# Turning tokens to channels by SyncE transfers of 32-partition squares and two full-width transposes, with weight rows read in that order

## Chip, cores and metric

One core of one Trainium2 chip. The time is that of the device in microseconds (us), as the median of runs of the whole kernel. Engines are named as the profile names them: PE is TensorE, DVE is VectorE, ACT is ScalarE, POOL is GpSimd, SP is SyncE, the engine whose instruction queue issues nearly all transfers here.

## What is computed

One layer of a hybrid decoder block on 256 tokens with 2048 channels, in fp32. Three branches (windowed attention, a pooling mixer, a state-space mixer) come from one input projection, are projected back and merged by gates; an output projection, a gated feed-forward layer of 5632 channels and a last norm follow. Of the reference, the part that the change touches:

```
y = ssd(...)                                            # 256 x 2048
g = (y * silu(z)).reshape(b, l, 4, 512)
g = g * rsqrt(mean(g * g, -1) + EPS)
ssm = g.reshape(b, l, 2048) * ssm_norm_w
merged = gates0 * (att @ w_attn_br) + gates1 * (pool @ w_pool_br) + gates2 * (ssm @ w_ssm_br)
x = x + merged @ w_out
h2 = rmsnorm(x, ln2_w)
gu = h2 @ w_gate_up
x = x + (silu(gu[..., :D_FF]) * gu[..., D_FF:]) @ w_down
return rmsnorm(x, final_w)
```

## The kernel before

**Products.** A product is computed with tokens on the output partitions (`tokens_block`): the operand with channels on its partitions is the stationary side, 128 channels by 128 tokens, and the weights stream by in blocks of 512 columns. One block of a product over 2048 channels takes 16 channel tiles, k = 0 to 15. Precision comes from splitting both sides in a high and a low fp32r part; `three` issues three matmuls for each pair, high by high (L201), high by low weights (L202) and low operand by high weights (L203). With two token tiles that is 96 matmuls of 512 columns a block. The weights of a block come in four loads of 1 MB (`weights`, L150, tile `raw`, four buffers), four channel tiles each. Each load is split in two pieces: ACT rounds a piece to `whi` (L139), DVE subtracts to get `wlo` (L140). There are five buffers of `whi` and of `wlo`, so a piece is split when PE has left the fifth piece before it.

**Turns.** What comes out of a product has tokens on its partitions. Before it can be the operand of the next product it has to be turned, tokens to channels. For a block of 256 tokens by 512 channels (four channel tiles) `turn` does this on DVE: 16 stream transposes, each of 32 partitions by 256 elements (L347), into `tt`, then a split of `tt` into the high and low tiles of the operand. Where a norm's vector multiplies the operand the split is by channel tile with the vector as a per-partition factor (L142 on ACT, L143 on DVE). There are 23 turns: four of `y` into `ssm`, four of `m` into `mp`, four of `x2` into `x2p`, and eleven of `ff` into `f`, in three parts of 4, 4 and 3 blocks (`FF_PARTS`). The last turn of an operand gives its last four channel tiles: k = 12 to 15, or 8 to 11 in the third part.

**Order of work.** The program order on each engine is that of a scheduler which starts from the order of the code. A turn isn't put where it is written: its steps are `tasks` with a charge in microseconds (`later`), and each piece of a running product lets one task go when enough charge has been saved (`side`). `soon` makes two tasks of the squares where an operand is wanted early.

**After a turn.** `w_out` follows the branch product, four blocks (`mp` as operand); gate and up products follow, eight blocks for each part but the last (`x2p`), then the `down` products of the part (`f`). So the first block that uses an operand starts as soon as the block before it ends, and comes to the last four channel tiles after three loads.

Of the kernel before, what the change touches and what calls it, by code (L numbers as in the profile page):

```python
# [10 lines left out]
F32 = mybir.dt.float32  # L11
# [60 lines left out]
def hybrid_block(ctx: ExitStack, tc: tile.TileContext, ins, out):  # L72
# [13 lines left out]
    def k4(shape, dt=F32, name="k4"):  # L86
        return work.tile([P, *shape], dt, tag="k4", name=name, bufs=21)
# [29 lines left out]
    def later(fn, cost=0.0):  # L117
        tasks.append((fn, cost))
# [27 lines left out]
    def weights(loads, shape, pieces=2):  # L146

        raw = wpool.tile([P, *shape], F32, tag="raw", name="raw", bufs=4)
        for to, src in loads:
            sp.dma_start(to(raw), src)  # L150
        n, cols = shape
        parts = []
        for h in range(pieces):
            a, b = h * (n // pieces), (h + 1) * (n // pieces)
            hi = wpool.tile([P, b - a, cols], F32R, tag="whi", name="whi", bufs=5)
            lo = wpool.tile([P, b - a, cols], F32R, tag="wlo", name="wlo", bufs=5)
            split(raw[:, a:b], hi, lo)
# [20 lines left out]
    class Parts:  # L180

        def __init__(self, n, name):
            self.t = [
                (k4([4, SEQ], F32R, f"{name}_hi"), k4([4, SEQ], F32R, f"{name}_lo")) for _ in range(n // 4)
            ]

        def hi(self, k):
            return self.t[k // 4][0][:, k % 4, :]  # L190
# [14 lines left out]
    def tokens_block(a, nk, loads_of, cols, loaded=None):  # L205

        accs = [acc() for _ in range(T)]
        step = 8 if cols <= 256 else 4
        for i in range(0, nk, step):
            n = min(step, nk - i)  # L210
            pieces = weights(loads_of(i, n), [n, cols])
            if loaded is not None:
                loaded(i)
            for s, e, hi, lo in pieces:
                for t in range(T):
                    tok = slice(t * P, (t + 1) * P)
# [59 lines left out]
    vec = k2([2, P], F32, name="vec")  # L276
    r0 = 0
    VEC = {}
    for name, n in (("ln2_w", 16), ("ssm_norm_w", 16), ("pool_scale", 8), ("conv_b", 24)):
        VEC[name] = r0, n  # L280
        r0 += n
    n_vec = r0
# [52 lines left out]
                    last = split(p[:, k, :], dst.hi(kt), dst.lo(kt), scale(kt))  # L335
        return last

    def turn(block, k0, dst, scale=None, soon=False):

        tt = k4([4, SEQ], F32, "tt")  # L340
        src = block.rearrange("p t (k j c) -> p t k j c", k=4, j=4)
        to = tt.rearrange("p k (t i s) -> p t k i s", t=T, i=4)

        def squares(rows_):
            for i in rows_:
                for j in range(4):
                    dve.transpose(to[32 * j:32 * j + 32, :, :, i, :], src[32 * i:32 * i + 32, :, :, j, :])  # L347

        def parts():
            if scale is None:  # L350
                hi, lo = dst.t[k0 // 4]
                split(tt, hi, lo)
            else:
                for k in range(4):
                    split(tt[:, k, :], dst.hi(k0 + k), dst.lo(k0 + k), scale(k0 + k))

        if soon:
            later(lambda: squares((0, 1)), 2.0)
# [32 lines left out]
    upto_rows = dram.tile([T, SSM_HEADS, P], F32, name="upto_rows")  # L391
    rst = const.tile([P, SEQ], F32, name="rst")

    for name in ("ln2_w", "ssm_norm_w", "pool_scale", "conv_b"):
        vec_load(name)
    pool.dma_start(vec[:96, 1, :], ins["conv_w"][0].rearrange("k (a c) -> (k a) c", c=P))
    for i, name in enumerate(("dt_bias", "a_log", "d_skip")):
        pool.dma_start(heads[:, i, :], ins[name][0].partition_broadcast(P))
    pool.dma_start(sink, ins["attn_sink"][0].partition_broadcast(P))
    pool.dma_start(cst, ins["cst"][:, P:])  # L400


    def vdt_loads(i, n):
# [352 lines left out]
            act.activation(sg[:, t, :], a, AF.Sigmoid, scale=rstd1[:, t:t + 1])  # L756
        return sg

    def branch(br, j, a_parts, w, sg):
        if br == 0:  # L760
            m4.append(k4([T, NB], F32, "m"))
        nk = w.shape[0] // P
        for t, a in enumerate(tokens_block(a_parts, nk, plain_loads(w, 0, j * NB, NB), NB)):
            if br == 0:
                dve.tensor_tensor(m4[j][:, t, :], a, sg[:, t, :], ALU.mult)
            else:
                dve.tensor_tensor(sg[:, t, :], a, sg[:, t, :], ALU.mult)
                (dve if br == 2 else pool).tensor_tensor(m4[j][:, t, :], m4[j][:, t, :], sg[:, t, :], ALU.add)
# [63 lines left out]
    for g in range(GROUPS):  # L832
        for t, a in enumerate(tokens_block(h, KD, plain_loads(w_in, 0, C_Z + g * NB, NB), NB)):
            sz = k2([NB], F32, "sz")
            act.activation(sz, a, AF.Silu, scale=rstd1[:, t:t + 1])
            dve.tensor_tensor(ys[g][:, t, :], ys[g][:, t, :], sz, ALU.mult)
            junk = k2([NB], F32, "junk")
            act.activation(junk, ys[g][:, t, :], AF.Square, accum_out=ssg[:, t, g:g + 1])

        def finish(g=g):  # L840
            rstd = rsqrt(ssg[:, :, g], NB, [T], "rsg")
            for t in range(T):
                dve.tensor_scalar(ys[g][:, t, :], ys[g][:, t, :], rstd[:, t:t + 1], None, ALU.mult)

        later(finish, 1.5)
        turn(ys[g], 4 * g, ssm, lambda k: vcol("ssm_norm_w", k))

    sg_ssm = [gate(2, j) for j in range(2)]
    finish_tasks()
    for j in range(4):  # L850
        branch(2, j, ssm, ins["w_ssm_br"][0], sg_ssm[j])
        if j + 2 < 4:
            sg_ssm.append(gate(2, j + 2))
        if j == 1:
            mp = Parts(KD, "mp")
            for i in range(2):
                turn(m4[i], 4 * i, mp)
        elif j > 1:
            turn(m4[j], 4 * j, mp, soon=j == 3)


    x2 = []
# [4 lines left out]
    ss2 = tiny([T, 4], "ss2", 1)  # L867
    x2p = Parts(KD, "x2p")
    for j in range(4):
        for t, a in enumerate(tokens_block(mp, KD, plain_loads(ins["w_out"][0], 0, j * NB, NB), NB)):  # L870
            dve.tensor_tensor(x2[j][:, t, :], a, x2[j][:, t, :], ALU.add)
            junk = k2([NB], F32, "junk")
            act.activation(junk, x2[j][:, t, :], AF.Square, accum_out=ss2[:, t, j:j + 1])
        turn(x2[j], 4 * j, x2p, lambda k: vcol("ln2_w", k), soon=j == 3)
    ssum2 = tiny([T], "ssum2", 1)
    dve.tensor_reduce(ssum2, ss2, AX.X, ALU.add)
    rstd2 = rsqrt(ssum2, D, [T], "rs2")
# [21 lines left out]
    for some in FF_PARTS:  # L899
        f = Parts(4 * len(some), "f")  # L900
        for i, b in enumerate(some):
            a_ = k4([T, NB], F32, "ff")
            for t, a in enumerate(tokens_block(x2p, KD, plain_loads(wgu, 0, b * NB, NB), NB)):
                act.activation(a_[:, t, :], a, AF.Silu, scale=rstd2[:, t:t + 1])
            if b == FB - 1:

                act.activation(tiny([1], "junk1"), a_[:, 1, :1], AF.Square)
                act.activation(tiny([1], "junk1"), rstd2[:, :1], AF.Sqrt)
            for t, a in enumerate(tokens_block(x2p, KD, plain_loads(wgu, 0, DFF + b * NB, NB), NB)):
                dve.scalar_tensor_tensor(  # L910
                    a_[:, t, :], a, rstd2[:, t:t + 1], a_[:, t, :], ALU.mult, ALU.mult
                )
            turn(a_, 4 * i, f, soon=i == len(some) - 1)
        k0, nk = 4 * some[0], 4 * len(some)
        last = some[-1] == FB - 1
        for j in range(3 if last else 4):
            down(j, 0, NB, j if last else None, tokens_block(f, nk, plain_loads(wd, k0, j * NB, NB), NB))
    down(3, 0, 256, 3, tokens_block(f, nk, plain_loads(wd, k0, 3 * NB, 256), 256))


    wl = []
    for i in range(0, nk, 8):
        n = min(8, nk - i)
        raw = wpool.tile([P, n, 256], F32, tag="raw", name="raw", bufs=4)
        sp.dma_start(raw, rows(wd, k0 + i, n, 3 * NB + 256, 256))
        for b in range(0, n, 4):
            hi, lo = k4([4, 256], F32R, "wl_hi"), k4([4, 256], F32R, "wl_lo")
            split(raw[:, b:b + 4], hi, lo)
            wl.append((hi, lo))
# [53 lines left out]
```

## Time and profile before

| | |
|---|---|
| time, median of 3 runs | 1661.74 us (1661.23 to 1662.84) |
| the profiled execution: time, span | 1662.78 us, 1661.0 us |
| granted clock of PE in it | 0.998 |
| PE busy | 1645.3 us, 99%, 7815 matmuls |
| DVE busy | 1140.2 us, 69% |
| ACT busy | 823.6 us, 50% |
| POOL busy | 58.9 us, 4% |
| SP's transfers (queue q1) | 183872 packets, 309.87 MB, 56.5% of 16 DMA engines |

The span is that of the instructions of one execution; the time of the same execution is 1.8 us longer. Busy shares are means over stages that differ. A transfer counts for its queue, not for the engine that issues it, and SP's own time in issuing isn't in the table.

### The profile page before, as it was taken

How to read it: one execution, taken by the hardware profiler on the slowest of the kernel's cores; microseconds unless marked ns; L12 is line 12 of the kernel's file. 1: busy time of each engine (PE TensorE's matmuls, PEld its weight loads, DVE VectorE, ACT ScalarE, POOL GpSimd, SP SyncE). 2: the span in 40 equal slices, each digit the busy share in tenths (PEclk: the TensorE clock that was granted, in tenths of full speed). 3: DMA queues.
4: the chain of work that ended last, by engine and by line, in shares of the span. 5: the costliest groups of instructions: out<-in, count | busy, mean ns of one | idle time of the engine just before them, and what ended most of it. 6: DMA issues, size and time to landing. Idle time of an engine off the chain costs nothing.

```text
span 1661.0 us, 20077 instructions
## 1 busy us (share of the span) xinstructions
PE 1645.3 (99%) x7815; PEld 1372.4 (83%) x7815; DVE 1140.2 (69%) x1598; ACT 823.6 (50%) x1073; POOL 58.9 (4%) x58
## 2 busy tenths in 40 slices
PE   8999999999999999999999999999999999999997
PEld 7888888888888888888888888888888888888887
DVE  5789898955754469844898866665556666446675
ACT  5467678544444456644445544443344444344443
POOL 1000001200210000000000000000000000000000
PEclk9999999999999999999999999999999999999999
DMA  9654655556565645656575555556556655555552
GB/s 273 203 166 144 198 190 192 177 178 190 167 216 189 202 154 201 225 181 200 170 253 197 185 203 184 184 192 210 201 178 203 202 186 194 201 183 199 195 172 89
DMA packets 186271, 316.68 MB, mean 191 GB/s; under 512 B 7644, under 2 KB 59104, under 8 KB 186176
## 3 DMA queue, kind: packets, MB, share of 16 engines
q1 hardware_dynamic: 183872, 309.87, 56.5%
q0 software_dynamic: 1552, 4.66, 1.0%
q8 instruction: 61, 1.00, 0.2%
q10 hardware_dynamic: 752, 0.86, 0.2%
q14 instruction: 34, 0.28, 0.0%
HBM read 313.25 MB, written 2.13 MB: 190 GB/s over the span
## 4 chain that ended last, share of the span: by engine, by line
PE 94%; DVE 4%; ACT 1%; DMA 1%; issue 1%; DVEq 0%; ACTq 0%
PE acc L203 26%; PE acc L201 26%; PE acc L202 26%; PE acc L234 9%; PE acc L235 4%; DVE tt L347 2%; DVE wlo L140 1%; PE sm L708 1%; PE tr L557 0%; ACT whi L139 0%; PE sm L234 0%; DMA raw<-in_w_in_dram 0%; PE sm L600 0%; PE tr L589 0%; PE sm L235 0%
## 5 line engine op out<-in xcount | busy, mean ns | idle before, releaser
L140 DVE TENSOR_TENSOR wlo<-raw,whi 128x1024 fp32r<-128x1024 f32 (+2 forms) x584 | 703.6, 1218 | 438.3 <-ACT whi L139 436.3
L139 ACT CAST whi<-raw 128x1024 fp32r<-128x1024 f32 (+2 forms) x584 | 604.1, 1039 | 664.7 <-PE acc L203 598.1
L201 PE MATMUL acc<-whi,x2p_hi 128*128 128x512 f32 x704 | 273.9, 389 | 0.0
L202 PE MATMUL acc<-wlo,x2p_hi 128*128 128x512 f32 x704 | 273.9, 389 | 0.0
L203 PE MATMUL acc<-whi,x2p_lo 128*128 128x512 f32 x704 | 273.9, 389 | 0.0
L234 PE MATMUL acc<-h,whi 128*128 128x512 f32 x640 | 227.6, 399 | 0.0
L201 PE MATMUL acc<-whi,h 128*128 128x512 f32 (+1 forms) x544 | 210.5, 388 | 2.3 <-ACT h L142 1.3
L202 PE MATMUL acc<-wlo,h 128*128 128x512 f32 (+1 forms) x544 | 208.6, 384 | 0.0
L203 PE MATMUL acc<-whi,h 128*128 128x512 f32 (+1 forms) x544 | 207.8, 384 | 0.1
L235 PE MATMUL acc<-h,wlo 128*128 128x256 f32 x640 | 180.1, 281 | 0.0
L201 PEld LDWEIGHTS acc<-whi,x2p_hi 128*128 128x128 f32 x704 | 132.1, 188 | 27.5
L203 PEld LDWEIGHTS acc<-whi,x2p_lo 128*128 128x128 f32 x704 | 132.1, 188 | 27.4
L202 PEld LDWEIGHTS acc<-wlo,x2p_hi 128*128 128x128 f32 x704 | 132.1, 188 | 27.4
L234 PEld LDWEIGHTS acc<-h,whi 128*128 128x128 f32 x640 | 120.1, 188 | 29.4 <-issue 1.8
L203 PE MATMUL acc<-whi,f_lo 128*128 128x512 f32 (+1 forms) x352 | 134.5, 382 | 0.4 <-DVE f_lo L140 0.4
L202 PE MATMUL acc<-wlo,f_hi 128*128 128x512 f32 (+1 forms) x352 | 134.4, 382 | 0.0
L201 PE MATMUL acc<-whi,f_hi 128*128 128x512 f32 (+1 forms) x352 | 134.4, 382 | 0.0
L235 PEld LDWEIGHTS acc<-h,wlo 128*128 128x128 f32 x640 | 120.8, 189 | 1.8 <-issue 1.8
L201 PEld LDWEIGHTS acc<-whi,h 128*128 128x128 f32 x544 | 101.9, 188 | 24.3 <-ACT h L142 2.3
L202 PEld LDWEIGHTS acc<-wlo,h 128*128 128x128 f32 x544 | 102.1, 188 | 21.1 <-issue 0.7
L203 PEld LDWEIGHTS acc<-whi,h 128*128 128x128 f32 x544 | 101.6, 188 | 20.7 <-DVE h L143 0.3
L347 DVE STREAM_TRANSPOSE tt<-ff 32x256 f32<-32x256 f32 x176 | 76.8, 436 | 2.6
(244 smaller groups left out, 1768.1 us busy)
## 6 DMA issues: line engine op xcount, KB each, us to landing
raw<-in_w_in_dram SPq DMA_DIRECT2D x104, 1024.0 KB, 5.2
raw<-in_w_gate_up_dram SPq DMA_DIRECT2D x88, 1024.0 KB, 5.1
raw<-in_w_down_dram SPq DMA_DIRECT2D x43, 1024.0 KB, 5.1
raw<-in_w_ssm_br_dram SPq DMA_DIRECT2D x16, 1024.0 KB, 5.1
raw<-in_w_out_dram SPq DMA_DIRECT2D x16, 1024.0 KB, 5.3
raw<-in_w_attn_br_dram SPq DMA_DIRECT2D x8, 1024.0 KB, 5.0
raw<-in_w_pool_br_dram SPq DMA_DIRECT2D x8, 1024.0 KB, 5.1
mt<-upto_rows POOLq DMA_DIRECT2D x8, 512.0 KB, 5.2
```

What stands on the lines that cost most here:

```text
L139: a = act.copy(hi, src)
L140: b = dve.tensor_tensor(lo, src, hi.bitcast(F32), ALU.subtract)
L201: pe.matmul(o, lhsT=xh, rhs=yh, start=first, stop=False)
L202: pe.matmul(o, lhsT=xh, rhs=yl, start=False, stop=False)
L203: pe.matmul(o, lhsT=xl, rhs=yh, start=False, stop=last)
L234: pe.matmul(accs[c], lhsT=hi[:, j, cols], rhs=a.both(k), start=k == 0, stop=False)
L235: pe.matmul(accs[c][:, :SEQ], lhsT=lo[:, j, cols], rhs=a.hi(k), start=False, stop=k == KD - 1)
L347: dve.transpose(to[32 * j:32 * j + 32, :, :, i, :], src[32 * i:32 * i + 32, :, :, j, :])
L708: pe.matmul(p[:, i * HD:(i + 1) * HD], lhsT=mt[:, i, :], rhs=xdt[:, i, :], start=True, stop=True)
```

## The change

Each turn is done in another way. `turn` takes a further tile `mid`. As one task, SP issues 16 transfers within the chip's memory (L368 of the changed kernel), each of which carries a square of 32 tokens by 128 channels, for both token tiles, to 32 other partitions: 64 pieces of 512 bytes. A charged pause follows, then a task with two stream transposes of all 128 partitions (L373, one for each token tile, 512 elements a partition, whose input is read in steps of four elements) and the same split as before. After such a turn a partition holds other channels than before: channel tile k of a block of four has the channels 4p + k. So the weights of the four products that follow are loaded with four consecutive rows to each partition (`turned`), and the two norm vectors that multiply turned operands come by two POOL transfers of their own in that order (`norms`) and no longer through the table of vectors. The last loads of `down`, of 256 columns, are issued in halves. A product waits for the turn of its operand (`need`) by letting all tasks before it go. `soon` is gone.

```diff
+    def turned(w, k0, n, c0, cols):
+
+        return [
+            (b, w[(k0 + b) * P:(k0 + b + 4) * P, c0:c0 + cols].rearrange("(p k) c -> p k c", k=4))
+            for b in range(0, n, 4)
+        ]
+
+    def turned_loads(w, k0, c0, cols):
+        return lambda i, n: [
+            ((lambda r, b=b: r[:, b:b + 4, :]), src) for b, src in turned(w, k0 + i, n, c0, cols)
+        ]
...
+        def need(self, k):
+
+            while k // 4 in self.waiting:
+                tasks.popleft()[0]()
...
+            if isinstance(a, Parts):
+                a.need(i)
             pieces = weights(loads_of(i, n), [n, cols])
...
-    def turn(block, k0, dst, scale=None, soon=False):
-
-        tt = k4([4, SEQ], F32, "tt")
-        src = block.rearrange("p t (k j c) -> p t k j c", k=4, j=4)
-        to = tt.rearrange("p k (t i s) -> p t k i s", t=T, i=4)
-
-        def squares(rows_):
-            for i in rows_:
+    def turn(block, k0, dst, scale=None, wait=5.0):
+
+
+
+        mid = k4([4, T, P], F32, "mid")
+        dst.waiting.add(k0 // 4)
+
+        def move():
+            for i in range(4):
                 for j in range(4):
-                    dve.transpose(to[32 * j:32 * j + 32, :, :, i, :], src[32 * i:32 * i + 32, :, :, j, :])
+                    sp.dma_start(mid[32 * j:32 * j + 32, i], block[32 * i:32 * i + 32, :, j * P:(j + 1) * P])
 
         def parts():
+            tt = k4([4, SEQ], F32, "tt")
+            for t in range(T):
+                dve.transpose(
+                    tt.rearrange("p k (t i s) -> p t i k s", t=T, i=4)[:, t],
+                    mid[:, :, t].rearrange("p i (c k) -> p i k c", k=4),
+                )
             if scale is None:
                 hi, lo = dst.t[k0 // 4]
                 split(tt, hi, lo)
             else:
                 for k in range(4):
                     split(tt[:, k, :], dst.hi(k0 + k), dst.lo(k0 + k), scale(k0 + k))
-
-        if soon:
-            later(lambda: squares((0, 1)), 2.0)
-            later(lambda: squares((2, 3)), 2.0)
-        else:
-            for i in range(4):
-                later(lambda i=i: squares((i,)), 1.75)
-        later(parts, 1.2)
+            dst.waiting.discard(k0 // 4)
+
+        later(move)
+        pause(wait)
+        later(parts, 3.8)
...
     pool.dma_start(cst, ins["cst"][:, P:])
+
+    norms = const.tile([P, 2, KD], F32, name="norms")
+    for i, name in enumerate(("ssm_norm_w", "ln2_w")):
+        pool.dma_start(
+            norms[:, i].rearrange("p (b k) -> p b k", k=4),
+            ins[name][0].rearrange("(b p k) -> p b k", p=P, k=4),
+        )
...
-        for t, a in enumerate(tokens_block(mp, KD, plain_loads(ins["w_out"][0], 0, j * NB, NB), NB)):
+        for t, a in enumerate(tokens_block(mp, KD, turned_loads(ins["w_out"][0], 0, j * NB, NB), NB)):
...
-        turn(x2[j], 4 * j, x2p, lambda k: vcol("ln2_w", k), soon=j == 3)
+        turn(x2[j], 4 * j, x2p, lambda k: norms[:, 1, k:k + 1])
...
-            turn(a_, 4 * i, f, soon=i == len(some) - 1)
+            turn(a_, 4 * i, f)
...
-        sp.dma_start(raw, rows(wd, k0 + i, n, 3 * NB + 256, 256))
+        for b, src in turned(wd, k0 + i, n, 3 * NB + 256, 256):
+            sp.dma_start(raw[:, b:b + 4, :], src)
```

How the program order changes is shown at three places.

**First place: the start of `w_out`.** SP's program before, from the last loads of the branch product on; `x_7110` to `x_7116` are the four blocks of the residual `x2`, and four `raw` loads make a block:

```order
L150 DMA raw<-in_w_ssm_br_dram 128x4x512 x4
L150 DMA raw<-in_w_in_dram 128x4x512 x4
L150 DMA raw<-in_w_ssm_br_dram 128x4x512 x8
L150 DMA raw<-in_w_out_dram 128x4x512 x3
L865 DMA x_7110<-in_x_dram 128x2x512
L865 DMA x_7112<-in_x_dram 128x2x512
L865 DMA x_7114<-in_x_dram 128x2x512
L865 DMA x_7116<-in_x_dram 128x2x512
L150 DMA raw<-in_w_out_dram 128x4x512 x13
L150 DMA raw<-in_w_gate_up_dram 128x4x512 x32
```

SP's program of the changed kernel, from the last load of the branch product on:

```order
L150 DMA raw<-in_w_ssm_br_dram 128x4x512
L150 DMA raw<-in_w_out_dram 128x4x512
L368 DMA mid<-m 32x2x128 x16
L150 DMA raw<-in_w_out_dram 128x4x512 x2
L896 DMA x_7132<-in_x_dram 128x2x512
L896 DMA x_7134<-in_x_dram 128x2x512
L896 DMA x_7136<-in_x_dram 128x2x512
L896 DMA x_7138<-in_x_dram 128x2x512
L368 DMA mid<-m 32x2x128 x16
L150 DMA raw<-in_w_out_dram 128x4x512 x5
L368 DMA mid<-x_7132 32x2x128 x16
L150 DMA raw<-in_w_out_dram 128x4x512 x4
```

The first of the row of five is the fourth load of the first `w_out` block, with k = 12 to 15; it now stands behind the 16 transfers of the last `m`. From here on every turn has such a row of 16 between the loads.

DVE's program at the same place, before; `raw_7129`, `raw_7179`, `raw_7215` and `raw_7249` are the first four loads of `w_out`, `m_3702` is the last block of `m`, and the first two rows belong to the first load:

```order
L140 TENSOR_TENSOR wlo_7132<-raw_7129,whi_7131 128x1024
L140 TENSOR_TENSOR wlo_7136<-raw_7129,whi_7135 128x1024
L140 TENSOR_TENSOR wlo_7182<-raw_7179,whi_7181 128x1024
L140 TENSOR_TENSOR wlo_7186<-raw_7179,whi_7185 128x1024
L767 TENSOR_TENSOR sg_6619<-acc_6943,sg_6619 128x512
L767 TENSOR_TENSOR sg_6619<-acc_6944,sg_6619 128x512
L768 TENSOR_TENSOR m_3702<-m_3702,sg_6619 128x512 x2
L140 TENSOR_TENSOR wlo_7218<-raw_7215,whi_7217 128x1024
L347 STREAM_TRANSPOSE tt_7109<-m_3702 32x2x4x32 x16
L140 TENSOR_TENSOR wlo_7222<-raw_7215,whi_7221 128x1024
L140 TENSOR_TENSOR wlo_7252<-raw_7249,whi_7251 128x1024
L140 TENSOR_TENSOR mp_lo_6767<-tt_7109,mp_hi_6766 128x1024
```

DVE's program of the changed kernel, where `raw_7185` and `raw_7235` are the second and third loads of `w_out` and `mid_6962` and `mid_7131` hold the moved squares of the last two blocks of `m`:

```order
L373 STREAM_TRANSPOSE tt_7122<-mid_6962 128x4x4x32 x2
L140 TENSOR_TENSOR mp_lo_6778<-tt_7122,mp_hi_6777 128x1024
L140 TENSOR_TENSOR wlo_7188<-raw_7185,whi_7187 128x1024
L798 TENSOR_TENSOR sg_6632<-acc_6963,sg_6632 128x512
L140 TENSOR_TENSOR wlo_7192<-raw_7185,whi_7191 128x1024
L799 TENSOR_TENSOR m_3703<-m_3703,sg_6632 128x512
L798 TENSOR_TENSOR sg_6632<-acc_6964,sg_6632 128x512
L140 TENSOR_TENSOR wlo_7238<-raw_7235,whi_7237 128x1024
L799 TENSOR_TENSOR m_3703<-m_3703,sg_6632 128x512
L140 TENSOR_TENSOR wlo_7242<-raw_7235,whi_7241 128x1024
L373 STREAM_TRANSPOSE tt_7269<-mid_7131 128x4x4x32 x2
L140 TENSOR_TENSOR mp_lo_6780<-tt_7269,mp_hi_6779 128x1024
```

The transposes of the last `m` but one moved behind the splits of the first `w_out` load and ahead of those of its second load, and the two halves of the last `m` are written between the splits of the second and third loads.

**Second place: the first `down` product of a part.** DVE's program before, from the split of the third `ff` turn of the part to the first result of `down`:

```order
L140 TENSOR_TENSOR f_lo<-tt,f_hi 128x1024
L140 TENSOR_TENSOR wlo<-raw,whi 128x1024 x14
L910 SCALAR_TENSOR_TENSOR ff<-acc,rs_r,ff 128x512 x2
L347 STREAM_TRANSPOSE tt<-ff 32x2x4x32 x16
L140 TENSOR_TENSOR wlo<-raw,whi 128x1024 x2
L140 TENSOR_TENSOR f_lo<-tt,f_hi 128x1024
L140 TENSOR_TENSOR wlo<-raw,whi 128x1024 x6
L890 TENSOR_TENSOR x_7110<-acc,x_7110 128x512 x2
```

DVE's program of the changed kernel over the same stretch:

```order
L140 TENSOR_TENSOR f_lo<-tt,f_hi 128x1024
L140 TENSOR_TENSOR wlo<-raw,whi 128x1024 x10
L941 SCALAR_TENSOR_TENSOR ff<-acc,rs_r,ff 128x512 x2
L140 TENSOR_TENSOR wlo<-raw,whi 128x1024 x5
L373 STREAM_TRANSPOSE tt<-mid 128x4x4x32 x2
L140 TENSOR_TENSOR wlo<-raw,whi 128x1024
L140 TENSOR_TENSOR f_lo<-tt,f_hi 128x1024
L140 TENSOR_TENSOR wlo<-raw,whi 128x1024 x2
L921 TENSOR_TENSOR x_7132<-acc,x_7132 128x512 x2
L140 TENSOR_TENSOR wlo<-raw,whi 128x1024 x8
```

Before, the last `ff` block was turned as soon as it was written; now five pieces of weights stand ahead of its two transposes, and one more between them and `f_lo`.

**Third place: the last part's first `down` product.** PE's program before, where `f_hi_11389` and `f_lo_11390` are the last four channel tiles (k = 8 to 11) and `acc_12277` and `acc_12278` the sums of the first block:

```order
L202 MATMUL acc_12278<-wlo_12336,f_hi_11387 128x512
L203 MATMUL acc_12278<-whi_12335,f_lo_11388 128x512
L201 MATMUL acc_12277<-whi_12367,f_hi_11389 128x512
L202 MATMUL acc_12277<-wlo_12368,f_hi_11389 128x512
L203 MATMUL acc_12277<-whi_12367,f_lo_11390 128x512
L201 MATMUL acc_12277<-whi_12367,f_hi_11389 128x512
```

PE's program of the changed kernel at this place, where the last four channel tiles are `f_hi_11450` and `f_lo_11451`, the first block's sums `acc_12344` and `acc_12345`, and the second block's `acc_12479` and `acc_12480`:

```order
L221 MATMUL acc_12479<-whi_12487,f_lo_11447 128x512
L219 MATMUL acc_12480<-whi_12487,f_hi_11446 128x512
L220 MATMUL acc_12480<-wlo_12488,f_hi_11446 128x512
L221 MATMUL acc_12480<-whi_12487,f_lo_11447 128x512
L219 MATMUL acc_12480<-whi_12487,f_hi_11446 128x512
L219 MATMUL acc_12344<-whi_12437,f_hi_11450 128x512
L220 MATMUL acc_12344<-wlo_12438,f_hi_11450 128x512
L219 MATMUL acc_12345<-whi_12437,f_hi_11450 128x512
L220 MATMUL acc_12345<-wlo_12438,f_hi_11450 128x512
L220 MATMUL acc_12480<-wlo_12488,f_hi_11446 128x512
L221 MATMUL acc_12480<-whi_12487,f_lo_11447 128x512
L221 MATMUL acc_12344<-whi_12437,f_lo_11451 128x512
```

Before, the last channel tiles followed directly on those with k = 4 to 7. Now 22 matmuls of the second block's first load (tile `f_hi_11446`, k = 0 to 3) stand ahead of the first matmul with the last tiles.

## Rows read from the trace of the kernel before

**Rows 1.** The head of the page: span, and the busy time of each engine.

```profile
span 1661.0 us, 20077 instructions
PE 1645.3 (99%) x7815; PEld 1372.4 (83%) x7815; DVE 1140.2 (69%) x1598; ACT 823.6 (50%) x1073; POOL 58.9 (4%) x58
```

**Rows 2.** Stretches: start:end, length, busy us of each engine, clock, DMA, GB/s.

```profile
0.00:50.00 50.00, 44.73 (x264) 39.02 (x265) 30.61 (x61) 30.70 (x56) 5.86 (x15) 1.00 0.91 272
...
900.00:1100.00 200.00, 200.00 (x884) 165.60 (x883) 139.39 (x187) 94.25 (x105) 0.00 (x0) 1.00 0.59 200
```

**Rows 3.** All waits of PE from 50 to 1652 us: us, times, longest.

```profile
PE acc L201 <- DVE sg L767: 0.8, 2, 0.4
PE acc L202 <- DVE wlo L140: 0.6, 1, 0.6
PE acc L203 <- DVE f_lo L140: 0.4, 1, 0.4
```

**Rows 4.** PE in order of time at two of its waits: start, us, instruction.

```profile
839.26 0.39 PE L201 MATMUL acc<-whi,ssm_hi 128*128 128x512 f32 x1
840.25 0.50 PE L202 MATMUL acc<-wlo,ssm_hi 128*128 128x512 f32 x1 [0.60 <-DVE wlo L140]
...
1596.57 0.39 PE L202 MATMUL acc<-wlo,f_hi 128*128 128x512 f32 x1
1597.37 0.50 PE L203 MATMUL acc<-whi,f_lo 128*128 128x512 f32 x1 [0.42 <-DVE f_lo L140]
```

**Rows 5.** PE in order of time: first matmuls with a new operand.

```profile
845.62 0.39 PE L201 MATMUL acc<-whi,mp_hi 128*128 128x512 f32 x1
...
932.66 0.39 PE L201 MATMUL acc<-whi,x2p_hi 128*128 128x512 f32 x1
...
1106.74 0.39 PE L201 MATMUL acc<-whi,f_hi 128*128 128x512 f32 x1
...
1585.46 0.39 PE L201 MATMUL acc<-whi,f_hi 128*128 128x512 f32 x1
```

**Rows 6.** DVE's groups by shape: count, busy us, mean ns, idle before.

```profile
L347 DVE STREAM_TRANSPOSE tt<-ff 32x256 f32<-32x256 f32 x176 | 76.8, 436 | 2.6
...
L242 DVE TENSOR_TENSOR cs<-acc,cs 128x256 f32<-128x256 f32 x40 | 16.3, 416 | 8.4 <-ACT cs L241 8.3
...
L140 DVE TENSOR_TENSOR f_lo<-tt,f_hi 128x1024 fp32r<-128x1024 f32 x11 | 13.4, 1217 | 0.0
...
L767 DVE TENSOR_TENSOR sg<-acc,sg 128x512 f32<-128x512 f32 x16 | 10.2, 681 | 0.0
```

**Rows 7.** ACT's groups by shape, columns as in Rows 6.

```profile
L139 ACT CAST whi<-raw 128x1024 fp32r<-128x1024 f32 x568 | 595.1, 1052 | 654.7 <-PE acc L203 594.3 <-PE acc L234 40.6 <-ACT whi L139 9.8
...
L142 ACT ACTIVATE x2p_hi<-tt,vecs 128x256 fp32r<-128x256 f32 x16 | 6.8, 498 | 7.2 <-DVE tt L347 7.2
```

**Rows 8.** SP's issues by line: ns least/median/most, first and last start.

```profile
L150 SPq DMA_DIRECT2D raw<-in_w_out_dram x16: 367/368/368, 821.7 to 903.7; - x16
...
L956 SPq DMA_DIRECT2D out_dram<-x x4: 383/404/423, 1651.4 to 1656.2; - x4
...
L883 SPq DMA_DIRECT2D fw<-in_final_w_dram x8: 332/511/1367, 160.9 to 174.3; - x8
```

**Rows 9.** Transfers: count, KB each, median us from issue to landing.

```profile
raw<-in_w_out_dram SPq DMA_DIRECT2D x16, 1024.0 KB, 5.3
...
upto_rows<-rows POOLq DMA_DIRECT2D x1, 32.0 KB, 1.9
```

**Rows 10.** ACT in order of time near the start of `w_out`.

```profile
845.82 1.06 ACT L139 CAST whi<-raw 128x1024 fp32r<-128x1024 f32 x1 [1.66 <-PE acc L203]
```

**Rows 11.** DVE in order of time at the first `down` product.

```profile
1106.45 1.40 DVE L910 SCALAR_TENSOR_TENSOR ff<-acc,rs_r,ff 128x512 f32<-128x512 f32 x2
1107.89 7.18 DVE L347 STREAM_TRANSPOSE tt<-ff 32x256 f32<-32x256 f32 x16
```

**Rows 12.** The DMA queue of SP's transfers: packets, MB, share of 16 engines.

```profile
q1 hardware_dynamic: 183872, 309.87, 56.5%
```

More of the change, by code (lines that the diff above doesn't have):

```diff
@@ L184, in __init__ @@
         def __init__(self, n, name):
+            self.waiting = set()
             self.t = [
@@ L278, in hybrid_block @@
     VEC = {}
-    for name, n in (("ln2_w", 16), ("ssm_norm_w", 16), ("pool_scale", 8), ("conv_b", 24)):
+    for name, n in (("pool_scale", 8), ("conv_b", 24)):
         VEC[name] = r0, n
@@ L392, in hybrid_block @@
     rst = const.tile([P, SEQ], F32, name="rst")
-    for name in ("ln2_w", "ssm_norm_w", "pool_scale", "conv_b"):
+    for name in VEC:
         vec_load(name)
@@ L757, in gate, with branch @@
         return sg
-    def branch(br, j, a_parts, w, sg):
+    def branch(br, j, a_parts, w, sg, loads=plain_loads):
         if br == 0:
@@ L762, in branch @@
         nk = w.shape[0] // P
-        for t, a in enumerate(tokens_block(a_parts, nk, plain_loads(w, 0, j * NB, NB), NB)):
+        for t, a in enumerate(tokens_block(a_parts, nk, loads(w, 0, j * NB, NB), NB)):
             if br == 0:
@@ L845, in hybrid_block @@
         later(finish, 1.5)
-        turn(ys[g], 4 * g, ssm, lambda k: vcol("ssm_norm_w", k))
+        turn(ys[g], 4 * g, ssm, lambda k: norms[:, 0, k:k + 1])
     sg_ssm = [gate(2, j) for j in range(2)]
@@ L850, in hybrid_block @@
     for j in range(4):
[L851 removed]
+        branch(2, j, ssm, ins["w_ssm_br"][0], sg_ssm[j], turned_loads)
         if j + 2 < 4:
@@ L858, in hybrid_block @@
         elif j > 1:
-            turn(m4[j], 4 * j, mp, soon=j == 3)
+            turn(m4[j], 4 * j, mp)
     x2 = []
@@ L902, in hybrid_block @@
             a_ = k4([T, NB], F32, "ff")
-            for t, a in enumerate(tokens_block(x2p, KD, plain_loads(wgu, 0, b * NB, NB), NB)):
+            for t, a in enumerate(tokens_block(x2p, KD, turned_loads(wgu, 0, b * NB, NB), NB)):
                 act.activation(a_[:, t, :], a, AF.Silu, scale=rstd2[:, t:t + 1])
@@ L908, in hybrid_block @@
                 act.activation(tiny([1], "junk1"), rstd2[:, :1], AF.Sqrt)
-            for t, a in enumerate(tokens_block(x2p, KD, plain_loads(wgu, 0, DFF + b * NB, NB), NB)):
+            for t, a in enumerate(tokens_block(x2p, KD, turned_loads(wgu, 0, DFF + b * NB, NB), NB)):
                 dve.scalar_tensor_tensor(
@@ L916, in hybrid_block @@
         for j in range(3 if last else 4):
-            down(j, 0, NB, j if last else None, tokens_block(f, nk, plain_loads(wd, k0, j * NB, NB), NB))
-    down(3, 0, 256, 3, tokens_block(f, nk, plain_loads(wd, k0, 3 * NB, 256), 256))
+            down(j, 0, NB, j if last else None, tokens_block(f, nk, turned_loads(wd, k0, j * NB, NB), NB))
+    down(3, 0, 256, 3, tokens_block(f, nk, turned_loads(wd, k0, 3 * NB, 256), 256))
     wl = []
```

## The prediction

> **What bounds the kernel now.** I read the page first: TensorE is busy for 1645.3 of 1661.0 us [rows 1]. The table by stretches then shows where the rest is: 5.3 us in the first 50 us, nothing from 900 to 1100 [rows 2], and the last nine microseconds, which hold only output. From 50 to 1652 us TensorE's waits are four: twice for `sg`, once for `wlo`, once for `f_lo` [rows 3]. In order of time the `wlo` one costs 840.25 − 839.26 less one matmul step of 0.23, so 0.76 (about 0.9 with the slower matmuls after it), and the `f_lo` one 0.57, about 0.7 likewise [rows 4]. All together they are under 3 us. So VectorE is not the limit, and freeing it can hardly win 0.2% of the time (3.3 us), which is about what a measurement of this kernel can tell from no change. The question is whether the longer route of a turn makes TensorE wait where it did not.
>
> TensorE's clock of work: between 932.66 and 1106.74 lie eight blocks of 16 channel tiles, 21.76 us each [rows 5]. A block is four loads, so a load lasts 5.44 us and each of its two pieces 2.72. ScalarE splits a piece when TensorE leaves the fifth piece before it, 0.2 us after that moment (845.82 for 845.62) [rows 5, 10]; the split costs 1.05 on ScalarE [rows 7], then about 1.2 on VectorE.
>
> **The change, term by term.** *Squares out.* 16 squares of 0.436 are 7.0 us of VectorE per turn, 161 us over 23 turns [rows 6]. The one wait that they cause by filling VectorE, at 839.26, should go: −0.9. The `sg` waits lie where no turn runs and stay.
>
> *Transposes in.* No transpose of 128 partitions is in the trace, nor one whose input steps by four elements. From below: a 32x256 square takes 436 ns and an ordinary 128x256 operation 416, so a transpose runs like any pass over as many columns, and 128x512 would be the 681 of `sg` [rows 6]. From above: it does the work of eight squares, 3.49. I take 1.3. The kernel's own charges are my reason: it charged 7.0 for 16 squares and 1.2 for the split, which the rows bear out (7.0 and 1.22) [rows 6], and it now charges 3.8 for two transposes and a split, 1.3 each, which lies between the ends.
>
> The trace cannot show that step's cost. [...]
>
> *The move.* 16 SyncE transfers of 32 KB. SyncE's issues take 0.37 for a weight load, 0.40 for an output row block, 0.33 to 1.37 (median 0.51) for `fw` [rows 8]; I take 0.41, 6.6 us for a move, bounds 5.3 and 8.2 by the 0.33 and the medians. Landing: 1.9, the one 32 KB transfer of such a kind [rows 9].
>
> A turn thus lasts 6.6 + 1.9 + 2.6 before its split where it lasted 7.2. Where its operand is used blocks later this is hidden behind those blocks of 21.76 us. That holds for the `y` turns, for `m` 0 and 1 and for all but the last `x2` and the last `ff` of each part. SyncE's own stay in these moves is hidden too: a load's issue takes it 0.37 us of each 5.44, and four raw buffers hold what TensorE needs meanwhile. The last turn of an operand is needed within three loads, 16.3 us after the first consumer starts; there the order of instructions decides.
>
> **A, w_out.** Before, SyncE went on to the load with tiles 12 to 15 at once; now that load stands behind the 16 transfers of the last `m`, and these wait for VectorE to write it. On VectorE the turn of `m` 2 now stands after the splits of the first `w_out` load, and so do those of its second. TensorE reaches `w_out` at 845.6 − 0.9 = 844.7. The load's second piece is split when the fourth piece before it ends, 836.6; + 0.2 + 1.05 + 1.2 = 839.1. From there VectorE and ScalarE are a chain: two transposes 2.6, `mp_hi` 1.05, `mp_lo` 1.22, then `wlo`, `sg`, `wlo`, `m`, `sg`, `wlo`, `m`, 3 × 1.22 + 4 × 0.68 = 6.4 [rows 6]: the last `m` is there at 850.4. Sixteen issues: 857.0. The load lands 5.3 later [rows 9], 862.3; the squares land at 858.9, transposes to 861.5, `mp_hi` to 862.5, `whi` to 863.6, `wlo` to 864.8. TensorE wants all this at 844.7 + 16.3 = 861.0, and two matmuls of 0.23 go ahead of the first with `wlo`: wait 3.3. With transposes of 0.68 the same chain gives 1.9.
>
> **B, first gate block.** It starts at 932.66; the move is issued 1.1 to 7.7 us later and landed at 9.6. The load concerned is ahead of the move here. VectorE has `wlo` of the next block's first piece ahead of the transposes: split at four pieces' end, 10.9 + 0.2 + 1.05 + 1.2 = 13.4, transposes to 16.0, four `x2p_hi` of 0.5 [rows 7] against a need at 16.3, and the next `wlo` before `x2p_lo`: wait 0.6 (none at 0.68).
>
> **C, the first `down` of parts 0 and 1.** Start 1106.74, last `ff` written at 1107.85 [rows 11], squares landed at 1116.4: 3.7 us before VectorE comes to them, since it now has the `wlo` of piece 8 first, until 1106.74 + 13.4 = 1120.1. Transposes to 1122.7, `f_hi` to 1123.75, a `wlo` and then `f_lo` to 1125.1. Need of `f_hi` 1123.07: 0.7; four matmuls later `f_lo` is 0.5 late. Wait 1.2, twice: 2.4. At 0.68 it is 0.1 each. Before, the squares came ahead of those `wlo` and were done at 1115.1 [rows 11].
>
> **D, the last part.** Start 1585.46 [rows 5]. The new order puts 22 matmuls of the next `down` ahead, so need is 1601.3 and not 1596.3. The `wlo` ahead of the transposes ends at 1585.46 + 13.4 = 1598.8, transposes to 1601.4, `f_hi` to 1602.45: wait 1.1 (none at 0.68); six matmuls later `f_lo` is just there. The old wait of 0.7 goes: net +0.4.
>
> *Weight rows, norm vectors, tail.* The weights come as the same bytes in the same 2 KB pieces, only from other rows: nothing; a load lands in 5.3 us and SyncE holds four buffers, 21.76 us of TensorE, as cover. The norm vectors are 1024 pieces of 16 bytes; at the 82 ns of an average packet (56.5% of 16 × 1661 us over 183872 [rows 12]) they would take 5.2 us of the 16 engines, at 91% load in those first 50 us [rows 2]: bounds 0 and 5.2, taken 0.4, since a small packet should cost less and nothing needs it soon. The two further loads at the end, 0.37 each, lie in SyncE's waits for buffers.
>
> Sum: −0.9 + 3.3 + 0.6 + 2.4 + 0.4 + 0.4 = +6.2. The profiled execution took 1662.78, 1.8 more than its span; against it 1669.0. It lies 1.0 above the median of the runs; from the median 1661.74 the forecast is 1667.9.
>
> **Rivals.** *The transposes cost a plain pass* (0.68; decides at B, C and D, where 1.2 us less ends all waits but 0.1): −0.9 + 1.9 + 0 + 0.2 − 0.7 + 0.4 = +0.9, 1662.6, no change. For it speaks that squares run like plain passes; against it the charge of 3.8. It turns at about 1.0 us per transpose, where the sum is 3.3. This is the rival on the other side: not slower.
>
> *SyncE is the new limit.* If a square takes 0.6 us instead of 0.41 (`fw` had 0.51, `x` loads more), each 0.1 adds 1.6 us at A, so 1671; up to there the 3.7 us of cover hides it at C and D. At 1.0 the landing comes 5.8 us after VectorE at B, C and D as well, and the sum is +38, 1700. For it: nothing in the trace sends 512-byte pieces from SBUF to SBUF. Against it: all of SyncE's rows but `fw` are near 0.4. [...]
>
> *Weight loads slow down* by the other row order. Only past 5.44 us per load would TensorE wait for them throughout; a load's packets take 512 × 82 ns over 16 engines, 2.6 us. Then any time over 1675.
>
> *Faster.* All four waits gone give back 2.6 us, 1659.1, still no measurable change; only the 5.3 us of the start could add to it, and nothing there speaks for that.
>
> **How the numbers follow.** Forecast 0.50, plain-pass transposes 0.34, SyncE as limit 0.10, slow loads 0.03, a gain 0.03. With the edge of the forecast that falls within 0.2% this makes faster 0.04, same 0.37, slower 0.59. Range 1661.5 to 1673: from the plain-pass case less a microsecond to SyncE at 0.6 with 2 us of norm packets on it; beyond lie the rest of SyncE's case, the loads and the gain. The forecast's own range is 1665 to 1670.
>
> **What would show it.** Right: transposes near 1.3 us, square issues near 0.4, new TensorE waits near 862, 949, 1123 and 1384 for `wlo`, `x2p`, `f_hi` and `f_lo`, none near 839, one of about 1 us some 16 us into the last part's first `down`. Wrong: transposes near 0.7, issues over 0.6, waits in blocks that hold no last turn, or a longer first 50 us.

## The result, and the profile after

The changed kernel takes 1677.02 us (1676.44 to 1677.13, 4 runs) against 1662.2 for the kernel before beside it: 1.0088 times, 95% interval 1.0076 to 1.0100, slower by 14.8 us. The forecast was 1667.9 with a range up to 1673. The sign was right, the size not.

The head of its page, which answers to [rows 1], shows VectorE 107 us less busy and TensorE no longer at 99%:

```profile
span 1675.1 us, 20245 instructions
PE 1649.6 (98%) x7815; PEld 1373.4 (82%) x7815; DVE 1033.6 (62%) x1276; ACT 823.8 (49%) x1073; POOL 59.3 (4%) x58
```

Cut at the first matmul of each new operand, the table by stretches (columns as in [rows 2]) gives `w_out`, the gate and up products of part 0, its `down`, and the last part's `down`:

```profile
843.94:942.87 98.93, 89.98 (x386) 73.53 (x385) 58.47 (x65) 43.82 (x59) 0.00 (x0) 0.95 0.65 218
942.87:1119.05 176.18, 174.66 (x769) 144.08 (x768) 99.45 (x96) 81.69 (x87) 0.00 (x0) 1.00 0.65 216
1119.05:1206.79 87.74, 87.65 (x385) 71.98 (x384) 47.17 (x44) 34.76 (x33) 0.00 (x0) 1.00 0.62 198
...
1599.16:1658.03 58.87, 57.89 (x289) 49.12 (x288) 36.95 (x45) 26.03 (x35) 0.00 (x0) 1.00 0.42 135
```

By [rows 5] `w_out` took 87.04 before and the gate and up products 174.08. So of the 14.1 us by which the span grew, `w_out` has 11.9 and the gate stage 2.1; each of the first two `down` stages has 0.7, the last 0.6 (58.31 before); and `w_out` starts 1.7 earlier than before. TensorE's waits from 50 us to its last matmul, which answer to [rows 3]:

```profile
PE acc L219 <- ACT whi L139: 8.9, 1, 8.9
PE acc L219 <- ACT x2p_hi L142: 1.3, 1, 1.3
PE acc L219 <- ACT f_hi L139: 1.0, 1, 1.0
PE acc L219 <- DVE sg L798: 0.8, 2, 0.4
PE acc L220 <- DVE wlo L140: 0.4, 1, 0.4
PE acc L221 <- DVE x2p_lo L143: 0.2, 1, 0.2
```

One wait holds most of the loss. Around it, TensorE in order of time:

```profile
860.03 0.39 PE L221 MATMUL acc<-whi,mp_lo 128*128 128x512 f32 x1
869.33 1.22 PE L219 MATMUL acc<-whi,mp_hi 128*128 128x512 f32 x2 [8.91 <-ACT whi L139]
870.59 0.80 PE L220 MATMUL acc<-wlo,mp_hi 128*128 128x512 f32 x1
...
872.04 0.63 PE L220 MATMUL acc<-wlo,mp_hi 128*128 128x512 f32 x1
872.47 0.63 PE L221 MATMUL acc<-whi,mp_lo 128*128 128x512 f32 x1
```

SyncE in order of time (a row is a run of issues, from the first's start to the last's end):

```profile
838.28 1.29 SPq L150 DMA_DIRECT2D raw<-in_w_out_dram  x2
839.62 2.89 SPq L896 DMA_DIRECT2D x<-in_x_dram  x4
851.31 10.61 SPq L368 DMA_DIRECT2D mid<-m  x16
862.02 10.22 SPq L150 DMA_DIRECT2D raw<-in_w_out_dram  x5
```

And ScalarE:

```profile
844.27 2.00 ACT L139 CAST whi<-raw 128x1024 fp32r<-128x1024 f32 x2 [1.56 <-DMA raw<-in_w_out_dram]
...
865.80 1.04 ACT L139 CAST mp_hi<-tt 128x1024 fp32r<-128x1024 f32 x1 [16.86 <-DVE tt L373]
868.23 1.99 ACT L139 CAST whi<-raw 128x1024 fp32r<-128x1024 f32 x2 [1.39 <-DMA raw<-in_w_out_dram]
```

The sixteen issues last from 851.31 to 861.92; then the load with tiles 12 to 15 is issued, and its split starts 6.2 us later. `mp_hi` was ready at 866.84: the load was the last to come. Behind the wait the matmuls step by 0.43 instead of 0.23 us. The stretches show why (length, TensorE busy and matmuls, granted clock, DMA share, GB/s):

```profile
860.00:862.00 2.00, 0.42 (x2) 1.00 0.22 49
...
864.00:866.00 2.00, 0.00 (x0) 0.60 0.97 282
866.00:868.00 2.00, 0.00 (x0) 0.50 1.05 380
...
872.00:874.00 2.00, 2.00 (x6) 0.50 1.05 389
874.00:876.00 2.00, 2.00 (x9) 0.84 1.06 390
```

After TensorE had been idle from 860.4 on, its granted clock fell to 0.50, and was back at 1.00, from 876 on, only after it had worked again from 869 to 875.

The prices, by line as in [rows 8] and for the transposes in the same columns:

```profile
L368 SPq DMA_DIRECT2D mid<-m x64: 585/595/1469, 795.4 to 861.3; - x64
L150 SPq DMA_DIRECT2D raw<-in_w_out_dram x16: 541/594/1010, 822.8 to 914.0; - x16
L150 SPq DMA_DIRECT2D raw<-in_w_gate_up_dram x88: 539/540/598, 921.2 to 1567.9; - x88
L373 DVE STREAM_TRANSPOSE tt<-mid x46: 1028/1077/1120, 622.2 to 1614.0; 128x512 f32<-128x512 f32 x46
```

An issue of a square takes 0.595 us, of a load in the new row order 0.54 (0.37 before, [rows 8]); a transpose takes 1.08.

### The profile page after: what moved, and what is told of

Read it like the earlier page. It is cut to its first block, busy times and chain, and to the rows that moved or that the text cites. A ratio compares the mean times of both kernels' runs of the same rounds, so it can differ in the third digit from the quotient of the medians.

```text
span 1675.1 us, 20245 instructions
## 1 busy us (share of the span) xinstructions
PE 1649.6 (98%) x7815; PEld 1373.4 (82%) x7815; DVE 1033.6 (62%) x1276; ACT 823.8 (49%) x1073; POOL 59.3 (4%) x58
## 4 chain that ended last, share of the span: by engine, by line
PE 86%; SPq 5%; DMA 3%; DVE 3%; ACT 2%; issue 1%; DVEq 0%; ACTq 0%
PE acc L221 23%; PE acc L219 23%; PE acc L220 23%; PE acc L254 9%; SPq L368 5%; PE acc L255 4%; DMA raw<-in_w_out_dram 2%; DVE wlo L140 1%; ACT whi L139 1%; PE sm L739 1%; DVE tt L373 1%; PE tr L588 0%; DMA raw<-in_w_in_dram 0%; PE sm L254 0%; PE sm L631 0%
## 5 line engine op out<-in xcount | busy, mean ns | idle before, releaser
L219 PEld LDWEIGHTS acc<-whi,f_hi 128*128 128x128 f32 x352 | 66.2, 188 | 15.0 <-ACT f_hi L139 2.3
```

Source lines behind the costliest of these rows:

```text
L219: pe.matmul(o, lhsT=xh, rhs=yh, start=first, stop=False)
```

## The experiments

Times of the kernel before beside each set: 1661.86 (for rows_only, mv_pool, tr_plain and warm), 1662.36 (mv_wide, ahead, hyb_m3 and warm40) and 1662.1 (mv_two and hyb2b). The theory after the result (theory 1): the loss is at the operands' last turns, where nothing covers SyncE's sixteen issues of 0.6 us, above all at `w_out`, where a weight load stands behind them. Rivals: the new row order makes loads slow (2), the squares' way is too long whoever issues them (3), bytes or packets cost and not issues (4).

**rows_only**, the kernel before with the new row order alone.

```diff
-        for t, a in enumerate(tokens_block(mp, KD, plain_loads(ins["w_out"][0], 0, j * NB, NB), NB)):
+        for t, a in enumerate(tokens_block(mp, KD, turned_loads(ins["w_out"][0], 0, j * NB, NB), NB)):
...
```

> The kernel before with nothing changed but the order of the weight rows in the four products (four consecutive rows to a partition, last loads in halves), so that weight rows and operand channels do not belong together: only its time counts. Theory 2 (that order makes loads slow): w_out's loads at 8 us instead of 5.3 and 5 us or more of new waits, 1667 or more. Theory 1: loads at 5.1 to 5.3 us, waits as before, 1662, no change.

1662.45 us, ratio 1.0002 (0.9993 to 1.0011). TensorE's waits are those of [rows 3], although the issue of these loads became dearer and `w_out`'s landed in 5.6 us:

```profile
L150 SPq DMA_DIRECT2D raw<-in_w_out_dram x16: 539/540/551, 819.7 to 901.7; - x16
```

Theory 2 falls: the order of rows alone brings no new wait. The median of 8.0 us for `w_out`'s loads in the changed kernel goes with their being issued in groups behind the moves: the first of a group landed in 5.7 to 6.1 us there, and each of those behind it took 2.0 us more.

**mv_wide**, four transfers of 128 partitions per turn.

```diff
             for i in range(4):
-                for j in range(4):
-                    sp.dma_start(mid[32 * j:32 * j + 32, i], block[32 * i:32 * i + 32, :, j * P:(j + 1) * P])
+                sp.dma_start(mid[:, i], block[:, :, i * P:(i + 1) * P])
```

> The changed kernel with four transfers of 128 partitions per turn in place of the sixteen squares: the same bytes, but the squares don't change partitions, so the operands are wrong and only the time counts. Theory 1 (SyncE's issue time per transfer is the cost): an issue of 0.4 to 0.6 us each, 2 to 2.4 us per move instead of 10; the load at w_out comes 8 us earlier and the wait there falls from 9 to 1 us or less, no low clock, and the smaller waits at gate, down and the last down shrink by what the squares' landing has in them: 1663 to 1666. If bytes or packets set the cost and not the number of issues (theory 4): a move still takes about 10 us and nothing changes, 1676.

1660.47 us, ratio 0.9989 (0.9980 to 0.9999). Its only listed wait from 50 us on is the old one for `sg`; a move, and the price of an issue:

```profile
PE acc L219 <- DVE sg L797: 0.8, 2, 0.4
...
845.68 2.65 SPq L367 DMA_DIRECT2D mid<-m  x4
...
L367 SPq DMA_DIRECT2D mid<-m x16: 600/629/826, 794.9 to 847.7; - x16
```

With four times the bytes an issue costs 0.63 us, where a square's cost 0.595: the price goes by the number of transfers. Theory 4 falls. That these transfers stay on their partitions isn't what saves the time, since an issue costs about the same either way (0.63 and 0.595 us). The other parts of the change (transposes, rows, norm vectors) hurt nothing measurable in this run.

**ahead**, all four loads of the first `w_out` block issued ahead of the last move of `m`.

```diff
+            if j == 3:
+                raws = [
+                    fetch(turned_loads(ins["w_out"][0], 0, 0, NB)(i, 4), [4, NB]) for i in (0, 4, 8, 12)
+                ]
             turn(m4[j], 4 * j, mp)
...
```

> The changed kernel with one thing moved: all four loads of the first w_out block are issued by SyncE ahead of the sixteen transfers of the last m (before: the fourth behind them). It splits theory 1 in two. The load alone (theory 1a): with it in time the wait at w_out goes altogether, and the low clock with it, 12 us less, 1665. The squares alone (theory 1b): the last m is written about 7.3 us after w_out starts, sixteen issues of 0.6 take 10, landing 1.9, transposes 2.1, mp_hi 1.1, so mp_hi comes about 5 us after its need whatever the load does: the wait falls from 9 to about 5, is for mp_hi instead of whi, and the clock drops for less or not at all; about 1671.

1673.35 us, 3.7 less than the changed kernel. TensorE now waits for the squares:

```profile
859.90 0.39 PE L226 MATMUL acc<-whi,mp_lo 128*128 128x512 f32 x1
866.99 0.79 PE L224 MATMUL acc<-whi,mp_hi 128*128 128x512 f32 x1 [6.70 <-ACT mp_hi L139]
```

So theory 1b: of 9.1 us (869.33 − 860.03 less a step) the load's place made 2.2; 6.9 is the squares' own lateness, and the clock fell with this wait as well (0.50 from 864 to 870). The wait is 2 us longer than expected. `w_out` is 2.9 us shorter than in the changed kernel, and the gate stage is back at 174.08: the last `x2` is added 2.2 us earlier in it, and its squares come in time.

**mv_pool**, all squares issued by POOL.

```diff
-                    sp.dma_start(mid[32 * j:32 * j + 32, i], ...
+                    pool.dma_start(mid[32 * j:32 * j + 32, i], ...
```

> The changed kernel, but the 368 transfers of squares are issued by POOL and not by SyncE. Theory 1 (SyncE's queue: sixteen issues of 0.6 us stand ahead of the load with tiles 12 to 15 of the first w_out block, and the load comes late): that load is issued as early as in the kernel before and TensorE no longer waits for whi there; what is left is the squares' own way, sixteen issues of POOL at 0.55, landing 1.9, two transposes 2.1 and mp_hi 1.05 after the last m, some 13.8 us against a need 9 to 10 us after it: a wait of about 4 us instead of 9, and little or no low clock behind it; about 1669. Theory 2 (the new order of the weight rows makes the loads slow, 8.0 us at w_out): the loads still take 8 us, no gain, 1675 or more. Theory 3 (the way of the squares alone is too long, whoever issues them): the wait keeps its 9 us, 1676.

1699.0 us, against every theory's number. At `w_out` it did what theory 1 said: the wait is 5.4 and for `mp_hi`, not for the load. But the squares' landing has a median of 4.1 us here instead of 1.9, VectorE stands at its transposes for them (107 us in all, 41 in the changed kernel), and `wlo` comes late in blocks that had no wait before, most of all during the `y` turns (7.3 of the 9.4 us):

```profile
PE acc L220 <- DVE wlo L140: 9.4, 6, 2.9
PE acc L219 <- ACT x2p_hi L142: 5.8, 1, 5.8
PE acc L219 <- ACT mp_hi L139: 5.4, 1, 5.4
PE acc L219 <- ACT f_hi L139: 4.1, 1, 4.1
```

Against the kernel before, 10 us are lost ahead of the branch product, 8 at `w_out`, 12 in the gate stage and 5 from the last part's `down` on. Why squares land later from POOL stays open. Theory 3 is half right: the way of the squares is too long by itself, though SyncE's is the shorter one.

**mv_two**, half of each move by ScalarE's queue.

```diff
-                    sp.dma_start(mid[32 * j:32 * j + 32, i], ...
+                    (sp if i < 2 else act).dma_start(mid[32 * j:32 * j + 32, i], ...
```

> The changed kernel with half of each move issued by SyncE and half by ScalarE's own queue; in this order of the program the load with tiles 12 to 15 is ahead of the last m's move. Theory 1 (0.6 us per issue, on one engine, is what makes the squares late): eight issues of 0.6 in place of sixteen, 5 us less in the chain after the last m, so of the 6.9 us wait for mp_hi that was left with the load ahead some 2 us stay, and the clock need not fall: 1664 to 1667. If the transfers themselves (landing, a shared path) are the limit: the issues or landings stretch to about twice and the wait stays near 6.9 us, 1673. What speaks against it: ScalarE's splits queue behind its issues, up to 5 us, which may give new waits for whi.

1689.94 us, a miss. The last `m`'s move took 9.4 us again, since SyncE waited in it for a weight load to land, and ScalarE's half took 8.4:

```profile
859.56 9.42 SPq L368 DMA_DIRECT2D mid<-m  x8
...
859.56 8.40 ACTq L368 DMA_DIRECT2D mid<-m  x8
...
SPq L368 <- DMA raw<-in_w_out_dram: 4.0, 1, 4.0
```

ScalarE's splits stood behind its own issues, with new waits for `whi` of up to 4.9 us. The wait for `mp_hi` fell to 1.3 us, but the last `m` was there 2.5 us after `w_out`'s start here and not 7.3, so this doesn't test the expected 2. The moves of `m`, `x2` and `ff` all lasted 8.6 to 11.9 us, because SyncE's issues waited for earlier transfers to land (37.6 us in all for squares of `ff`). Whether eight issues alone would do it stays open. Only the moves of `y` show a clear saving from the second queue, 6.0 to 7.0 us for 10.2 to 11.1 in the changed kernel; neither this run nor mv_pool was faster.

**tr_plain**, transposes with a contiguous read.

```diff
-                    mid[:, :, t].rearrange("p i (c k) -> p i k c", k=4),
+                    mid[:, :, t].rearrange("p i (k c) -> p i k c", k=4),
```

> The changed kernel, but the two transposes of a turn read their input in contiguous runs of 32 elements instead of steps of four, so the channels of a tile do not belong to its weight rows: only its time counts. The price of the stepped read by itself: if it is what makes a transpose 1.08 us, the transposes fall to about 0.7, 0.8 us off each turn, which shows at the four late turns alone: about 3 us, 1674. Theory 1 and 2 expect the wait of about 9 us at w_out to stay nearly whole. If the transposes keep 1.08, no change.

1675.34 us, 1.7 less where about 3 were expected; the wait at `w_out` stays (from 859.73 to 869.20). Each of the first two `down` stages is 0.5 us shorter than in the changed kernel, but the gate stage is 1.8 longer, since the clock fell behind its wait (0.50 from 962 to 964), which it didn't in the changed kernel (1.00 in the same stretch).

```profile
L373 DVE STREAM_TRANSPOSE tt<-mid x46: 668/688/715, 622.6 to 1613.5; 128x512 f32<-128x512 f32 x46
```

0.688 is the plain pass of the prediction's bound, 1.077 the price with steps: the stepped read took 1.57 times as long.

**hyb_m3**, the last `m` by sixteen squares on VectorE, read in steps of four.

```diff
-            turn(m4[j], 4 * j, mp)
+            turn(m4[j], 4 * j, mp, squares_=j == 3)
...
```

> The changed kernel with the last turn of m alone done on VectorE again, by sixteen square transposes that read in steps of four so that the new order of channels holds. Theory 1: no SyncE issues ahead of the load, no wait at w_out and no low clock, all other places as in the changed kernel: 12 us less, 1665. A square may cost more than 0.436 with its stepped read: up to 0.7, 11 us for sixteen, which the 9 us before the need would not quite hide: then 2 us more, 1667.

1673.14 us, 6 worse than the worse guess. The squares take 10.1 us with that read, and begin 9.6 us after `w_out`'s start, 4.8 before the change, because the turn before still goes by SyncE; `mp_hi` is waited for 4.4 us:

```profile
853.13 10.13 DVE L368 STREAM_TRANSPOSE tt<-m 32x256 f32<-32x256 f32 x16
```

Nor were the other places as in the changed kernel: the gate stage takes 178.65 us, 2.5 more, with a wait of 2.2 for `x2p_hi` and a slow clock behind it (0.50 from 958 to 960).

**warm and warm40**, 80 and 40 matmuls on constants put into the wait.

```diff
+            if warm == i:
+                keep_warm(WARM)
...
```

> The changed kernel with 80 further matmuls of 128 columns on constants, nearly all of them put just ahead of the first matmul with tiles 12 to 15 of the first w_out block, about 8.5 us of work that nobody reads. Theory 1 with the clock (TensorE idles there for 9 us, its granted clock falls to half, and the matmuls after it are slow until it rises): the work lies inside the wait, the clock stays at 1.0, and the matmuls behind it keep 0.23 us: 2 to 2.5 us faster than the changed kernel, about 1674.7. If the low clock costs nothing, because something else sets the pace there (the loads, theory 2): no change or slightly slower, 1677 to 1678.

> As the run with 80 further matmuls, with 40: the 80 took 17 us and outlasted the wait, 40 should take about 8.5 and end within it. With the clock held at 1.0 the matmuls after the wait keep 0.23 us: 2 to 2.5 us faster than the changed kernel, 1674.7. If the low clock costs nothing: 1677.

1680.31 and 1678.94 us. Each such fp32 matmul runs as two instructions (160 matmuls more in the trace for the 80, 80 for the 40), so the 80 outlasted the wait. The 40 fit, and the clock stayed at 1.0, with transfers as dense as in the same stretch of the changed kernel:

```profile
861.42 8.20 PE L293 MATMUL sm<-ones 128*128 128x128 f32 x72
869.43 0.50 PE L220 MATMUL acc<-whi,mp_hi 128*128 128x512 f32 x1
870.69 0.50 PE L221 MATMUL acc<-wlo,mp_hi 128*128 128x512 f32 x1 [0.76 <-DVE wlo L141]
...
872.00:874.00 2.00, 2.00 (x10) 1.00 1.05 394
...
957.43 0.39 PE L222 MATMUL acc<-whi,x2p_lo 128*128 128x512 f32 x1
960.85 0.50 PE L220 MATMUL acc<-whi,x2p_hi 128*128 128x512 f32 x1 [3.03 <-ACT x2p_hi L143]
...
962.64 0.63 PE L221 MATMUL acc<-wlo,x2p_hi 128*128 128x512 f32 x1
963.06 0.63 PE L222 MATMUL acc<-whi,x2p_lo 128*128 128x512 f32 x1
```

So it is the clock that makes the matmuls slow, and not the transfers beside them. But for one wait for `wlo` they step by 0.23, and from the end of the wait to the gate stage it takes 71.9 us instead of 73.5: 1.6 saved. The other part of the loss behind the wait is that `wlo`, which the slow matmuls had partly hidden. The 1.6 us are given back: TensorE reaches the gate stage's wait earlier, but `x2p_hi` comes at the same moment (960.85 here, 960.64 in the changed kernel), because the squares of `x2` set it. The wait grew from 1.5 to 3.2 us, the clock fell behind it (steps of 0.42 from 962.6 on), and the `down` product starts 1.8 us later than in the changed kernel. So removing the low clock at `w_out` alone wins nothing: the run is 1.9 us slower.

**hyb2b**, the version the runs point to: the last two turns of `m`, the last of `x2` and the last `ff` of each part by VectorE's squares with plain rows for those tiles, all others, those of `y` among them, by SyncE.

```diff
-            turn(m4[j], 4 * j, mp)
+            turn(m4[j], 4 * j, mp, squares_=j >= 2)
...
-            turn(a_, 4 * i, f)
+            turn(a_, 4 * i, f, squares_=i == len(some) - 1)
...
```

> A mixture of both kernels: the last turn of each operand (and of m the last two) is done by VectorE's sixteen squares as in the kernel before, with plain weight rows for those four channel tiles; all other turns go by SyncE and two full-width transposes. Theory 1 (the whole loss lies at the operands' last turns, where sixteen issues have no cover; elsewhere the moves are hidden): no wait at w_out, gate and the first two down products, the wait near 839 gone, that of the last down as before: 1660.5 to 1662, a gain of up to 1.5 us or none. Rival (the moves hurt elsewhere too, by late loads): waits in blocks that hold a move, 1664 or more.

1662.01 us, ratio 0.9998 (0.9989 to 1.0007). The loss is gone altogether, with 17 of the 23 turns still done by SyncE:

```profile
PE acc L224 <- DVE sg L827: 0.8, 2, 0.4
PE acc L225 <- DVE wlo L140: 0.6, 1, 0.6
PE acc L226 <- DVE f_lo L140: 0.4, 1, 0.4
```

The `wlo` wait is now one near 704, in the stage of the `y` turns, where the changed kernel has its 0.4 too; that is all the moves cost elsewhere. The version doesn't beat the kernel before: only 3 us of waits were to be had.

## Why the prediction was wrong

The bound on any gain held: the best time of all was 1660.47. So did the place of the waits: `w_out`, gate, two `down`, the last `down`, and none near 839; only the 0.4 near 704, in a block that holds a `y` turn, wasn't foreseen. What failed is a term, A, forecast at 3.3 and measured at 11.9 (98.93 − 87.04). By its own steps:

- "I take 0.41": an issue took 0.595, 0.66 with what lies between, so the load was issued 10.8 us after the last `m` (862.0 − 851.2) instead of 6.6, +4.2. The rows that I went by were transfers to and from DRAM in plain order; the bound of 8.2 from above was too low.
- "The last `m` is there" 5.7 us after `w_out`'s start: it was 7.3 (851.2 − 843.9), +1.6. ScalarE waited for `w_out`'s second load (the row at 844.27), which stood behind the move of the turn before, and that move had itself waited 2.6 us for a load to land. I had counted what queues behind the last move, not behind the one ahead of it.
- "The load lands 5.3 later": 6.2, +0.9, with four more loads right behind it. With 0.9 less after the landing, since this wait ended with `whi` and what `wlo` cost lies in the next item, that makes the wait 9.1.
- Not in the sum at all: TensorE's clock behind the wait, 0.50 from 866 to 874. The matmuls behind it lost 2.8 us, of which 1.6 came back with the clock held (warm40).

The squares' own way fails by the first two of these steps as well: with the load issued ahead of the move, they were still 6.9 us late (ahead).

The other terms: B 2.1 for 0.6, because the last `x2` is added later (its move begins 3.4 us into the stage, not 1.1) and the move is longer; C 1.4 for 2.4, with transposes of 1.08 for 1.3. D came to 0.6 for 0.4 by another way than forecast: its squares landed after VectorE was ready for them, 13.8 us into the stage. The wait at 839 went as forecast. The first matmul of `w_out` is earlier by 1.7, of which 0.9 is that wait; the norm vectors, charged at 0.4, show no loss.

Of the rivals "SyncE is the new limit" was the case, at its price of 0.6. It had been given 1671 and one chance in ten: the sum at that price left out the earlier move and the clock. The plain-pass rival is refuted by the 1.08 of the changed kernel against 0.69 in tr_plain, and slow loads by rows_only.

## What to carry to other kernels

When work moves from an engine with room to a queue, cost the queue by instructions and not by bytes (here 0.595 us to issue a transfer of 32 KB, 0.63 for one of 128 KB), and look for every load that stands behind those instructions, the one behind the turn before included. Here such a chain was all but free wherever its product is needed a block later (hyb2b, 1662.01 us against 1662.1), and cost in full at the last piece of an operand (11.9 us at `w_out`), so the two kinds of place deserve two ways of doing it. A wait like the 9.1 us at `w_out`, behind which the granted clock was 0.50, is to be priced with that clock, here 1.6 us, and what is saved there may only be waited for at the next such place.

## What was not expected of the hardware

The issue of a load of the same 1 MB in the same 2 KB pieces took 0.37 us with one row of each channel tile to a partition and 0.54 with four consecutive rows; that of a transfer within the chip's memory took 0.595 with 32 partitions and 0.63 with 128. POOL issued squares at 0.54, but they landed after a median of 4.1 us, SyncE's after 1.9. A stream transpose of 32x256 went from 0.436 to 0.618 us with a read in steps of four, one of 128x512 from 0.688 to 1.077.
